# Token-major projections with a transposed hand-over in a two-layer hybrid encoder

## The chip, the core and the metric

The kernel runs on one core of a Trainium2 chip. The metric is the device time of one execution in microseconds (us); of the kernel before, three runs were timed and the median counts. The engines, as the profile names them: PE is TensorE's matrix multiply and PEld its weight load, DVE is VectorE, ACT is ScalarE, POOL is GpSimd, and SP is the queue that issues nearly all transfers.

## The reference

Two residual layers over 256 tokens of 2048 features, all in float32. Layer 0 mixes tokens by attention (16 query heads, 4 key/value heads, RMS-normed and rotated), layer 1 by a recurrence with a convolution of width 4 in front and a gate branch beside it. Behind each mixer stands a gated feed-forward with 5632 hidden features.

```python
def rms_norm(x, g):
    y = xf * lax.rsqrt(jnp.mean(xf * xf, axis=-1, keepdims=True) + EPS)
    return (y * g).astype(x.dtype)

def recurrent_mixer(h, w_in, conv_w, conv_b, w_a, b_a, w_i, b_i, lam, w_out):
    xb, yb = jnp.split(h @ w_in, 2, axis=-1)
    yb = jax.nn.gelu(yb, approximate=True)
    xb = depthwise_conv_centred(xb, conv_w, conv_b)
    h_fwd = rg_lru(xb, ..., reverse=False)
    h_bwd = rg_lru(xb, ..., reverse=True)
    return ((h_fwd + h_bwd) * yb) @ w_out

def swiglu(h, w_gate, w_up, w_down):
    return (jax.nn.silu(h @ w_gate) * (h @ w_up)) @ w_down

for i in range(2):
    x = x + mixer[i](rms_norm(x, norm_mix[i]))
    x = x + swiglu(rms_norm(x, norm_ffn[i]), w_gate[i], w_up[i], w_down[i])
```

## The kernel before

**Number format.** Each float32 operand is split into a rounded high part and the rest: `hi` and `lo` of a weight, and the two halves `xh|xl` of an activation tile (256 + 256 columns for 256 tokens). A product is hi x xh + hi x xl + lo x xh. Weights come in halves of eight 128x128 blocks (512 KB) on SP (`load_half`, L108); ScalarE casts them to `hi` (L114) and VectorE subtracts to get `lo` (L115). The pools `raw`, `hi` and `lo` hold five halves each.

**Feature-major projections.** Activations and the residual `x_sb` are stored with features on the partitions. `blocks` (L203) holds a weight block stationary and streams the activations: one matmul of 512 columns (hi by xh|xl) and one of 256 (lo by xh), whose two halves VectorE adds up (`evac`, `add_residual`). `project_sum` (L230 to L232) sums within the accumulator by three matmuls of 256; the recurrence's input projection uses it.

**Token-major projections.** `project_tokens` (L222) holds 128 tokens of the activations stationary and streams 512 weight columns. Only layer 1's down projection uses it. For that the residual is turned to token-major: 16 transposes of VectorE (L604) and 16 transfers (L608), spread through the first units of the feed-forward.

**Feed-forward.** The 44 blocks of 128 hidden features go in parts of 16, 14 and 14. `unit` makes one block: gate, scale by 1/rms, Silu, scale (GpSimd, L632), up, product. After each part its down projection adds to the residual; one unit of the next part goes ahead of it.

**Norm.** When a block of the residual is done, ScalarE scales it by the gain (L310), VectorE makes the low part (L313), GpSimd squares and sums (L322, L324). When all are done, `finish` (L333) sums over the partitions by four matmuls with ones and takes 1/rms, which is applied after the projection.

**What sets the order.** TensorE's instructions stand in the order in which the program is written. `later(t, fn)` puts a piece of small work t steps of the running projection ahead. On the other engines a scheduler orders the instructions, and tile pools set the waits.

Of the kernel before, what the change touches and what calls it, by code (L numbers as in the profile page):

```python
# [18 lines left out]
P = 128  # L19
S = 256  # L20
# [7 lines left out]
PARTS = [16, 14, 14]  # L28
HALF = 8
WIDE = 512  # L30
COMMON = {"ss", "sq", "nv", "nr", "rsq_t", "fg", "fu"}
# [4 lines left out]
FRONT = 4  # L36
HELD = 3
# [32 lines left out]
def trunk(ctx, tc, w, out):  # L70
# [10 lines left out]

    uid = [0]
# [39 lines left out]
    def out_order(src):  # L122
        both = [halves(src[j], KT) for j in range(KT)]
        return [both[j][i] for i in range(2) for j in range(FRONT)] + sum(both[FRONT:], [])

    def ffn_order(l):
        at = np.cumsum([0] + PARTS)
        units = [sum((halves(w[f"w_{m}{l}"][i], KT) for m in ("gate", "up")), []) for i in range(at[-1])]
        seq = units[: at[1]]
        for p, n in enumerate(PARTS):  # L130
            more = units[at[p + 1] : at[p + 2]] if p + 1 < len(PARTS) else []
            src = w[f"w_down{l}_{p}"]
            if l:
                down = [[(src[c, i], HALF) for c in range(4) for i in range(n // 2)]]
            else:
                down = [halves(src[j], n) for j in range(KT)]
                if not more:
                    down[:2] = [down[j][i : i + 1] for i in range(2) for j in range(2)]
            seq += more[:1] + down + more[1:]
        return sum(seq, [])  # L140
# [3 lines left out]
    order += out_order(w["w_o"]) + ffn_order(0)  # L144
    for b in range(-1, NBLK):
        xin = range(2 * b + 2, 2 * b + 4) if b + 1 < NBLK else []
        yin = range(KT + 2 * b, KT + 2 * b + 2) if b >= 0 else []
        order += sum((halves(w["w_in"][c], KT) for c in (*xin, *yin)), [])
    order += out_order(w["w_out"]) + ffn_order(1)
# [63 lines left out]
    def project_tokens(xs):  # L213
        accs = [new_acc() for _ in range(2)]
        for k0 in range(0, len(xs), 2):
            half()
# [16 lines left out]

    def project_sum(xs):
        bank = new_acc()
        acc = bank[:, :S]
        for k0 in range(0, len(xs), HALF):
            for k, (hi, lo) in enumerate(half(), k0):
                three(acc, hi, lo, xs[k], k == 0, k == len(xs) - 1)
                step()  # L240
        return acc, bank[:, S:]

    def output(xs, ready, norm, close):
        accs = [new_acc() for _ in range(FRONT)]
        for acc in accs:
            blocks(acc, half(), xs, 0)
        late = [half() for j in range(HELD)]
        for acc, wt in zip(accs, late):
            blocks(acc, wt[: ready - HALF], xs, HALF)
        flush()  # L250
        close()
        for j in range(KT):
            if j < HELD:
                blocks(accs[j], late[j][ready - HALF :], xs, ready)
            elif j < FRONT:
                blocks(accs[j], half(), xs, HALF)
            acc = accs[j] if j < FRONT else project(xs)
            add_residual(j, acc, norm)
        norm.finish_later(NORM + 2)
# [15 lines left out]
    xq = [cst.tile([P, 4, S], F32, tag=f"x{k}", name=f"x{k}") for k in range(KT // 4)]  # L275
    x_sb = [xq[k // 4][:, k % 4, :] for k in range(KT)]
# [4 lines left out]
    cn = ap.tile([P, 2 * S + P], F32, tag="cn", name="cn", bufs=1)  # L281
# [7 lines left out]
    ident = cn[:, 2 * S :]  # L289
# [6 lines left out]
    class Norm:  # L296
        def __init__(self, gname, gofs):
            self.g = (gname, gofs)
            self.xs = []
            self.ss = tmp("ss", bufs=1)  # L300

        def add(self, k):
            self.scale(k)
            self.square(k, pool)

        def scale(self, k, eng=act):
            g = col(self.g[0], self.g[1] + k)
            t = xp.tile([P, 2 * S], F32R, tag="xg", name=nm("xg"), bufs=16)
            if eng is act:
                i = act.activation(t[:, :S], x_sb[k], AF.Copy, scale=g)  # L310
            else:
                i = eng.tensor_scalar(t[:, :S], x_sb[k], g, 1.0, ALU.mult, ALU.mult)
            dve.scalar_tensor_tensor(t[:, S:], x_sb[k], g, t[:, :S].bitcast(F32), ALU.mult, ALU.subtract)  # L313
            self.xs.append(t)
            return i

        def square(self, k, eng):
            sq = self.ss if k == 0 else tmp("sq", bufs=4)
            if eng is act:
                act.activation(sq, x_sb[k], AF.Square)  # L320
            else:
                eng.tensor_tensor(sq, x_sb[k], x_sb[k], ALU.mult)  # L322
            if k:
                pool.tensor_tensor(self.ss, self.ss, sq, ALU.add)  # L324

        def finish_later(self, delay=NORM):
            later(delay, self.finish)

        def finish(self):
            pst = ps_m.tile([P, 2 * S], F32, tag="pm", name=nm("pm"))  # L330
            for a in range(2):
                sl = slice(a * P, a * P + P)
                pe.matmul(pst[:, sl], ones, self.ss[:, sl], start=True, stop=True)  # L333
            self.v = tmp("nv", bufs=1)
            dve.tensor_scalar(self.v, pst[:, :S], 1.0 / D, EPS, ALU.mult, ALU.add)
            self.r = rsqrt(self.v, "nr")
# [12 lines left out]
    def add_residual(j, acc, norm):  # L349
        dve.tensor_tensor(x_sb[j], x_sb[j], acc[:, :S], ALU.add)  # L350
        dve.tensor_tensor(x_sb[j], x_sb[j], acc[:, S:], ALU.add)
        if norm is not None:
            norm.add(j)
# [23 lines left out]
    def scale_x(i):  # L377
        for k in range(2 * i, 2 * i + 2):
            j = n0.scale(k)
            if i:  # L380
                follow(j, newest["cast"])
# [9 lines left out]
    x_tok = ap.tile([P, 2, D], F32, tag="kv", name="x_tok", bufs=1)  # L391

    def token_squares(a):
        for i in range(2):
            t = x_tok[:, a, i * D // 2 : (i + 1) * D // 2]
            newest["cast"] = follow(act.activation(t, t, AF.Square, accum_out=msq[:, a, i : i + 1]), newest["cast"])  # L396

    def load_tables():
        sync.dma_start(out=cn, in_=w["cn"])
# [61 lines left out]
    def keys_values():  # L461
        kv = ap.tile([P, 2 * NKV, 2 * S], F32R, tag="kv", name="kv", bufs=1)
        kT.extend(kv[:, h, :] for h in range(NKV))
        vt.extend(kv[:, NKV + h, :].rearrange("p (a b d) -> p a b d", a=2, b=2) for h in range(NKV))
# [123 lines left out]
    def end_attention():  # L588
        decay_constants()
        at.close()  # L590
        scope.pop()

    nf = Norm("norm_ffn", 0)
    output(o_t, KT - 2, nf, end_attention)


    class Turned:
        def __init__(self):
            fp = ctx.enter_context(tc.tile_pool(name="fp", bufs=1))
            self.blocks = fp.tile([P, 8, KT, 32], F32, tag="xb", name="xb")  # L600
            self.x = fp.tile([P, 2, 4, WIDE], F32, tag="xt", name="xt")

        def turn(self, k):
            dve.transpose(self.blocks[:, :, k, :], x_sb[k])  # L604

        def move(self, i, j):
            src = self.blocks[32 * i : 32 * i + 32, j::4, :, :].rearrange("p a k r -> p a (k r)")
            sync.dma_start(out=self.x[32 * j : 32 * j + 32, :, i, :], in_=src)  # L608

        def add(self, c, accs, end):  # L610
            for a, acc in enumerate(accs):
                n = 2 if end and c == 3 else 1
                for i in range(n):
                    sl = slice(i * WIDE // n, (i + 1) * WIDE // n)
                    y = self.x[:, a, c, sl]
                    dve.tensor_tensor(y, y, acc[:, sl], ALU.add)
                    if end:
                        sync.dma_start(out=out[:, a, c, sl], in_=y)


    def ffn(l, norm, nxt):
        turned = Turned() if nxt is None else None
        moves = []
        if turned:
            moves = [partial(turned.turn, k) for k in range(KT)]
            moves += [partial(turned.move, i, j) for i in range(4) for j in range(4)]

        def unit(i):
            g = evac(project(norm.xs), "fg")
            dve.tensor_tensor(g, g, norm.r, ALU.mult)  # L630
            table_act(g, g, AF.Silu)
            pool.tensor_tensor(g, g, norm.r, ALU.mult)  # L632
            u = evac(project(norm.xs), "fu")
            dve.tensor_tensor(u, u, g, ALU.mult)
            h = act_tile()
            split(h, u)
            return h

        bounds = np.cumsum([0] + PARTS)
        hid = []  # L640
        for i in range(PARTS[0]):
            hid.append(unit(i))
            if i >= 2:
                for _ in range(3):
                    if moves:
# [237 lines left out]
```

## Time and profile before

| | |
|---|---|
| runs | 2060.05, 2060.22, 2060.23 us, median 2060.22 |
| profiled execution | 2060.85 us, its span 2059.1 us |
| granted TensorE clock | 1.00 |
| busy share PE, DVE, ACT, POOL | 100%, 69%, 52%, 19% |
| moved from and to memory | 388 MB, 189 GB/s |

The profile is one execution. Busy time is the time in which an engine executed something; the chain of waits follows the work that ended last backwards, so that its shares add up to the span. A row such as `L203 PE MATMUL ... x3200 | 1011.1, 395 | 0.3` gives line, engine, operation, count, busy time in us, mean of one in ns, and the idle time of the engine ahead of it. Matmuls overlap in their pipeline, so their pace is read from a stretch of them divided by their number, not from the mean of one.

### The profile page before, as it was taken

The numbers are of one execution on the slowest core, as the hardware profiler recorded it, in microseconds if no ns is written. First come the engines' busy times: TensorE is split into PE (matmuls) and PEld (weight loads), VectorE is DVE, ScalarE is ACT, GpSimd is POOL, SyncE is SP. The second block draws the span as 40 slices with busy tenths as digits, with TensorE's granted clock in tenths as the row PEclk, the third lists the DMA queues.
The fourth block names the chain that finished last, engine by engine and source line by source line (L and its number), as shares of the span: only waits on it lengthen the run. The fifth ranks groups of instructions, "written<-read, shape, count | busy, mean of one in ns | idle before, by whom it ended". The sixth has DMA issues, their size and how long they took to land.

```text
span 2059.1 us, 32056 instructions
## 1 busy us (share of the span) xinstructions
PE 2051.9 (100%) x12162; PEld 1812.3 (88%) x12162; DVE 1428.1 (69%) x2093; ACT 1069.0 (52%) x1597; POOL 391.1 (19%) x394
## 2 busy tenths in 40 slices
PE   9999999999999999999999999999999999999999
PEld 8898888888888888888999998888888888888887
DVE  7998876665566666668878879866654666556654
ACT  7666444443344434444589896544443444444442
POOL 1563611110011000113334433311100111001100
PEclk9999999999999999999999999999999999999999
DMA  8444655555555565556555545665555555555553
GB/s 315 160 137 140 223 189 187 192 185 193 186 191 187 177 193 200 187 181 185 199 177 178 193 149 197 203 215 190 189 193 195 186 191 187 194 194 185 190 201 130
DMA packets 111306, 388.43 MB, mean 189 GB/s; under 512 B 12592, under 2 KB 13232, under 8 KB 111024
## 3 DMA queue, kind: packets, MB, share of 16 engines
q1 hardware_dynamic: 111008, 386.36, 56.4%
q8 instruction: 96, 1.57, 0.3%
q14 instruction: 58, 0.48, 0.1%
q10 hardware_dynamic: 144, 0.02, 0.0%
HBM read 382.13 MB, written 2.10 MB: 187 GB/s over the span
## 4 chain that ended last, share of the span: by engine, by line
PE 95%; DVE 2%; DMA 1%; ACT 1%; issue 1%; POOL 0%; SPq 0%; DVEq 0%; POOLq 0%
PE acc L203 71%; PE acc L222 12%; PE acc L230 3%; PE acc L231 3%; PE acc L232 3%; PE pm L232 1%; DVE lo L115 1%; PE pm L230 1%; PE pm L231 1%; DMA x_tok<-in_xt_dram 1%; DMA raw<-in_w_k_dram 0%; PE pm L539 0%; ACT hi L114 0%; ACT x_tok L396 0%; PE pm L511 0%
## 5 line engine op out<-in xcount | busy, mean ns | idle before, releaser
L115 DVE TENSOR_TENSOR lo<-raw,hi 128x1024 fp32r<-128x1024 f32 (+1 forms) x716 | 885.3, 1237 | 384.7 <-ACT hi L114 378.7
L114 ACT CAST hi<-raw 128x1024 fp32r<-128x1024 f32 (+1 forms) x716 | 740.4, 1036 | 582.5 <-PE acc L203 265.7
L203 PE MATMUL acc<-xg,hi 128*128 128x512 f32 x3200 | 1011.1, 395 | 0.3 <-ACT hi L114 0.3
L203 PEld LDWEIGHTS acc<-xg,lo 128*128 128x128 f32 x3200 | 600.9, 188 | 141.1 <-DVE lo L115 2.2
L203 PE MATMUL acc<-xg,lo 128*128 128x256 f32 x3200 | 638.4, 279 | 0.7 <-DVE lo L115 0.6
L203 PEld LDWEIGHTS acc<-xg,hi 128*128 128x128 f32 x3200 | 489.9, 189 | 0.8 <-ACT hi L114 0.6
L203 PE MATMUL acc<-act,hi 128*128 128x512 f32 x1202 | 379.0, 395 | 0.0
L632 POOL TENSOR_TENSOR fg<-fg,nr 128x256 f32<-128x256 f32 x88 | 118.1, 1342 | 1182.6 <-ACT fg L364 1182.6
L203 PEld LDWEIGHTS acc<-act,lo 128*128 128x128 f32 x1202 | 225.8, 188 | 52.9
L203 PE MATMUL acc<-act,lo 128*128 128x256 f32 x1202 | 237.3, 278 | 0.0
L222 PE MATMUL acc<-hi,act 128*128 128x512 f32 x704 | 217.3, 389 | 0.0
L203 PEld LDWEIGHTS acc<-act,hi 128*128 128x128 f32 x1202 | 183.6, 189 | 0.0
L222 PEld LDWEIGHTS acc<-hi,act 128*128 128x128 f32 x704 | 132.1, 188 | 27.3
L230 PE MATMUL acc<-xg,hi 128*128 128x256 f32 x512 | 144.8, 283 | 0.0
L231 PE MATMUL acc<-xg,hi 128*128 128x256 f32 x512 | 144.6, 282 | 0.0
L232 PE MATMUL acc<-xg,lo 128*128 128x256 f32 x512 | 144.4, 282 | 0.0
L222 PE MATMUL acc<-lo,act 128*128 128x512 f32 x352 | 136.9, 389 | 0.0
L263 ACT COPY fg<-acc 128x256 f32<-128x256 f32 x88 | 32.8, 373 | 150.0 <-PE acc L203 149.8
L263 ACT COPY fu<-acc 128x256 f32<-128x256 f32 x88 | 32.8, 372 | 149.4 <-PE acc L203 149.4
L232 PEld LDWEIGHTS acc<-xg,lo 128*128 128x128 f32 x512 | 97.9, 191 | 0.0
L230 PEld LDWEIGHTS acc<-xg,hi 128*128 128x128 f32 x512 | 97.9, 191 | 0.0
L231 PEld LDWEIGHTS acc<-xg,hi 128*128 128x128 f32 x512 | 97.9, 191 | 0.0
(180 smaller groups left out, 1595.6 us busy)
## 6 DMA issues: line engine op xcount, KB each, us to landing
raw<-in_w_gate_dram SPq DMA_DIRECT2D x176, 512.0 KB, 3.4
raw<-in_w_up_dram SPq DMA_DIRECT2D x176, 512.0 KB, 3.4
raw<-in_w_down_dram SPq DMA_DIRECT2D x152, 512.0 KB, 3.3
raw<-in_w_in_dram SPq DMA_DIRECT2D x64, 512.0 KB, 4.0
raw<-in_w_qv_dram SPq DMA_DIRECT2D x40, 512.0 KB, 3.5
raw<-in_w_o_dram SPq DMA_DIRECT2D x32, 512.0 KB, 4.2
raw<-in_w_out_dram SPq DMA_DIRECT2D x32, 512.0 KB, 3.6
raw<-in_w_down_dram SPq DMA_DIRECT2D x32, 384.0 KB, 3.1
```

The costliest lines, as they stand in the source:

```text
L114: newest["cast"] = act.copy(hi[:, sl, :], raw[:, sl, :])
L115: dve.tensor_tensor(lo[:, sl, :], raw[:, sl, :], hi[:, sl, :].bitcast(F32), ALU.subtract)
L203: pe.matmul(o, w, x, start=(k == 0 and not part), stop=(k == total - 1 and not part))
L222: pe.matmul(accs[a], x, wt[:, k, :], start=(k0 + k == 0 and n == 0), stop=(end and k == 1 and n == 2))
L230: pe.matmul(o, hi, x[:, :S], start=start, stop=False)
L231: pe.matmul(o, hi, x[:, S:], start=False, stop=False)
L232: pe.matmul(o, lo, x[:, :S], start=False, stop=stop)
L263: i = act.copy(t, acc[:, S:])
L632: pool.tensor_tensor(g, g, norm.r, ALU.mult)
```

## The change

The residual `x_tok` is kept token-major throughout, and w_o, w_out, gate, up and down of both layers all go through `project_tokens` (L223 in the new file) in four, or eleven, columns of 512 features. Whatever has to be an operand of the next projection is brought back to features by `turned`: for 512 columns two transposes of 32x32 blocks on VectorE and 16 transfers from on-chip memory to on-chip memory of 32 KB, all on SP, or half on ScalarE's queue for the last columns ahead of a norm (`hurry`). The hidden features come out of a unit four blocks at a time, and the parts are 12, 16 and 16 blocks; no unit goes ahead of a down projection. The sums of squares are ScalarE's, by token; 1/rms goes into the Silu's scale and into the product. Only the recurrence's input projection stays feature-major, and needs 1/rms along the columns: `spread` multiplies a diagonal by ones. Its first two projections are interleaved (`project_two`), so that the last four operands come late in both.

```diff
-PARTS = [16, 14, 14]
+PARTS = [12, 16, 16]
...
+    def project_two(xs, late):
+        banks = [new_acc() for _ in range(2)]
+        for t in banks:
+            sums(t[:, :S], half(), xs, 0)
+        rest = [half() for _ in range(2)]
+        n = len(xs) - HALF - late
+        for t, wt in zip(banks, rest):
+            sums(t[:, :S], wt[:n], xs, HALF)
+        for t, wt in zip(banks, rest):
+            sums(t[:, :S], wt[n:], xs, HALF + n)
+            yield t[:, :S], t[:, S:]
...
+        def operand(self, x, wide=False):
...
+            i = act.activation(hi, x, AF.Copy, scale=g)
+            dve.scalar_tensor_tensor(lo, x, g, hi.bitcast(F32), ALU.mult, ALU.subtract)
...
+        def add(self, c):
+            for a in range(2):
+                act.activation(tmp("nj", (P, WIDE), bufs=1), x_tok[:, a, c, :], AF.Square, accum_out=self.sums[:, a, c : c + 1])
+            for f in turned(x_tok[:, :, c, :], c == NCOL - 1):
+                self.operand(f, True)
...
+        def spread(self):
+            dg = tmp("ndg", bufs=1)
             for a in range(2):
+                dve.tensor_scalar(dg[:, a * P : (a + 1) * P], ident, self.rt[:, a : a + 1], None, ALU.mult)
+
+            def stage():
+                pst = ps_m.tile([P, 2 * S], F32, tag="pm", name=nm("pm"))
+                for a in range(2):
+                    sl = slice(a * P, a * P + P)
+                    pe.matmul(pst[:, sl], ones, dg[:, sl], start=True, stop=True)
+                self.r = tmp("nrb", bufs=1)
+                act.copy(self.r, pst[:, :S])
+
+            later(NORM, stage)
...
+    def turned(src, hurry=False):
+        b = fp[0].tile([P, 2, FOUR, P], F32, tag="tb", name=nm("tb"))
+        f = fp[0].tile([P, 8, FOUR, 32], F32, tag="tf", name=nm("tf"))
+        for a in range(2):
+            dve.transpose(b[:, a, :, :], src[:, a, :])
+        for q in range(4):
+            for i in range(4):
+                (act if hurry and i % 2 else sync).dma_start(
+                    out=f[32 * i : 32 * i + 32, q::4, :, :].rearrange("f a k t -> f a (k t)"),
+                    in_=b[32 * q : 32 * q + 32, :, i, :],
+                )
+        return [f[:, :, k, :] for k in range(FOUR)]
...
+    def output(xs, norm=None, end=False, ready=0, close=None):
+        for c in range(NCOL):
+            accs = project_tokens(xs, ready, None if c else close)
...
+        def unit():
+            g, u = (fp[0].tile([P, 2, WIDE], F32, tag=t, name=nm(t), bufs=1) for t in ("fg", "fu"))
+            for a, acc in enumerate(project_tokens(norm.xs)):
+                table_act(g[:, a, :], acc, AF.Silu, scale=norm.rt[:, a : a + 1])
+            for a, acc in enumerate(project_tokens(norm.xs)):
+                dve.scalar_tensor_tensor(u[:, a, :], acc, norm.rt[:, a : a + 1], g[:, a, :], ALU.mult, ALU.mult)
+            for f in turned(u):
+                h = act_tile()
+                hi, lo = (h[:, o : o + S].rearrange("p (q t) -> p q t", t=32) for o in (0, S))
+                act.copy(hi, f)
+                dve.tensor_tensor(lo, f, hi.bitcast(F32), ALU.subtract)
+                yield h
+
         for p, n in enumerate(PARTS):
+            hid = [h for _ in range(n // FOUR) for h in unit()]
             last = p == len(PARTS) - 1
...
+            output(hid, nxt if last else None, last and nxt is None)
...
+            accs = (project_sum(nr.xs) for _ in range(2)) if blk else project_two(nr.xs, FOUR)
+            nxt.xcs = [conv_branch(2 * b + 2 + i, t) for i, t in enumerate(accs)]
```

The first place is the start of the recurrence. On VectorE (DVE) the rows before, around the step that turns the norm's sum `pm` into 1/rms `nr` (L335 to L346) and the first use of it in the convolution (L685), were these:

```order
L665 TENSOR_TENSOR x_78<-x_78,acc_10068 128x256
L115 TENSOR_TENSOR lo_10334<-raw_10332,hi_10333 128x1024
L313 SCALAR_TENSOR_TENSOR xg_10124<-x_78,pk,xg_10124 128x256
L335 TENSOR_SCALAR nv_10192<-pm_10189 128x256
L115 TENSOR_TENSOR lo_10364<-raw_10362,hi_10363 128x1024
L344 TENSOR_TENSOR rsq_t_10195<-nv_10192,nr_10194 128x256
L345 SCALAR_TENSOR_TENSOR rsq_t_10195<-rsq_t_10195,nr_10194 128x256
L346 SCALAR_TENSOR_TENSOR nr_10194<-rsq_t_10195,nr_10194 128x256
L685 TENSOR_TENSOR cb_10222<-acc_10149,nr_10194 128x256
```

In the changed kernel the last residual column's two transposes (L348) are followed by the norm's small steps, the low parts of the four operands `xg` made from the transferred `tf`, and the diagonal `ndg`:

```order
L117 TENSOR_TENSOR lo_8876<-raw_8874,hi_8875 128x1024
L322 TENSOR_REDUCE nrt_8665<-nsq_3258 128x2
L323 TENSOR_SCALAR nrt_8665<-nrt_8665 128x2
L117 TENSOR_TENSOR lo_8906<-raw_8904,hi_8905 128x1024
L368 TENSOR_TENSOR rsq_s_8669<-nrt_8665,nr_8668 128x2
L308 SCALAR_TENSOR_TENSOR xg_8653<-tf_8634,pk,xg_8653 128x256
L308 SCALAR_TENSOR_TENSOR xg_8656<-tf_8634,pk,xg_8656 128x256
L308 SCALAR_TENSOR_TENSOR xg_8659<-tf_8634,pk,xg_8659 128x256
L369 SCALAR_TENSOR_TENSOR rsq_s_8669<-rsq_s_8669,nr_8668 128x2
L308 SCALAR_TENSOR_TENSOR xg_8662<-tf_8634,pk,xg_8662 128x256
L370 SCALAR_TENSOR_TENSOR nr_8668<-rsq_s_8669,nr_8668 128x2
L330 TENSOR_SCALAR ndg_8676<-ident,nr_8668 128x128 x2
```

So 1/rms comes ahead of the matmuls of L336 and behind the four operands, where it came after the matmuls of L333 and apart from the operands. On TensorE the two matmuls of L336 stand 27 matmuls into the interleaved projections, at the same distance as L333 before:

```order
L231 MATMUL acc_8699<-xg_8101,hi_8731 128x256
L232 MATMUL acc_8699<-xg_8101,hi_8731 128x256
L233 MATMUL acc_8699<-xg_8101,lo_8732 128x256
L336 MATMUL pm_8739<-ndg_8676,ones 128x128 x2
L231 MATMUL acc_8699<-xg_8104,hi_8731 128x256
```

The second place is the first down projection of layer 0. On SP the 16 transfers `tf` of the part's last unit stand among the loads of the down weights, ten halves behind the last half of the up weights:

```order
L110 DMA raw_4363<-in_w_down_0_dram 128x1024
L110 DMA raw_4381<-in_w_down_0_dram 128x1024
L110 DMA raw_4399<-in_w_down_0_dram 128x1024
L110 DMA raw_4417<-in_w_down_0_dram 128x1024
L351 DMA tf_4218<-tb_4217 32x2x128 x16
L110 DMA raw_4435<-in_w_down_0_dram 128x1024
```

Before, SP had nothing but weight loads there. On TensorE the first operand `act_4237` made from them is used in the fifth half of the down weights, behind the eight operands of the two units ahead (here the end of the fourth):

```order
L223 MATMUL acc_4250<-hi_4306,act_3916 128x512
L223 MATMUL acc_4250<-lo_4307,act_3916 128x512
L223 MATMUL acc_4250<-hi_4306,act_3916 128x512
L223 MATMUL acc_4249<-hi_4324,act_4237 128x512
L223 MATMUL acc_4249<-lo_4325,act_4237 128x512
```

More of the change, by code (lines that the diff above doesn't have):

```diff
@@ L34 @@
 GRID_W = 64
-FRONT = 4
-HELD = 3
 WARM = 10
@@ L147, in trunk @@
         yin = range(KT + 2 * b, KT + 2 * b + 2) if b >= 0 else []
-        order += sum((halves(w["w_in"][c], KT) for c in (*xin, *yin)), [])
-    order += out_order(w["w_out"]) + ffn_order(1)
+        both = [halves(w["w_in"][c], KT) for c in (*xin, *yin)]
+        order += [t[i] for i in range(2) for t in both] if b < 0 else sum(both, [])
+    order += wide("w_out") + ffn_order(1)
     taken = [0]
@@ L232, in three, with sums @@
         pe.matmul(o, lo, x[:, :S], start=False, stop=stop)
+    def sums(acc, wt, xs, k0):
+        for k, (hi, lo) in enumerate(wt, k0):
+            three(acc, hi, lo, xs[k], k == 0, k == len(xs) - 1)
+            step()
     def project_sum(xs):
         bank = new_acc()
-        acc = bank[:, :S]
         for k0 in range(0, len(xs), HALF):
[L238 to L259, printed above, removed]
+            sums(bank[:, :S], half(), xs, k0)
+        return bank[:, :S], bank[:, S:]
+    def project_two(xs, late):
[9 more added lines that the diff above has]
+            yield t[:, :S], t[:, S:]
     def evac(acc, tag, after=None):
@@ L299, in __init__ @@
             self.xs = []
[L300 to L307, printed above, removed]
-            t = xp.tile([P, 2 * S], F32R, tag="xg", name=nm("xg"), bufs=16)
[L309 to L313, printed above, removed]
+            self.sums = tmp("nsq", (P, 2, NCOL))
@@ L591, in end_attention @@
         scope.pop()
+        open_ffn()
     nf = Norm("norm_ffn", 0)
[L594 to L618, printed above, removed]
@@ L621, in ffn @@
[L621 to L645, printed above, removed]
-                        moves.pop(0)()
+    output(o_t, nf, ready=KT - 2, close=end_attention)
```

169 lines of the change are left out of this document (78 added, 91 removed).

## The prediction

> **What bounds the kernel now.** I read the page first, for the engine that is never idle:
>
> ```profile
> PE 2051.9 (100%) x12162; PEld 1812.3 (88%) x12162; DVE 1428.1 (69%) x2093; ACT 1069.0 (52%) x1597; POOL 391.1 (19%) x394
> PEclk9999999999999999999999999999999999999999
> PE 95%; DVE 2%; DMA 1%; ACT 1%; issue 1%; POOL 0%; SPq 0%; DVEq 0%; POOLq 0%
> ```
>
> TensorE is busy in all of the span at the full clock, and the chain that ended last is 95% TensorE. So only the number and the pace of its matmuls count, until something makes it wait. The chain in order of time (start, length, what, how many instructions) gives the paces, and one window inside the recurrence the third:
>
> ```profile
> 273.46 0.44 PE pm L333 x4
> 273.90 726.99 PE acc L203 x4174
> ...
> 1514.83 87.06 PE acc L222 x384
> ...
> 1979.01 76.18 PE acc L222 x336
> ```
>
> ```profile
> 1060.00:1180.00 120.00, 120.00 (x1007) 120.00 (x1006) 102.44 (x167) 109.19 (x186) 45.48 (x58) 1.00 0.57 185
> ```
>
> L203 is the feature-major projection: per 128x128 weight block one matmul of 512 columns and one of 256, 2 x 726.99/4174 = 348.3 ns. L222 is the token-major one: 87.06/384 = 226.7 ns per matmul of 512. Four blocks side by side (128x512 weights) take three of them for each 128 of the 256 tokens, so six: 1.5 a block, 340.1 ns. The piece at 1979.01 agrees (76.18/336 = 226.7). The recurrence's input projection takes three matmuls of 256: 3 x 120.00/1007 = 357.5 ns. None of these stretches has a gap: 726.99 us of back-to-back matmuls cross every boundary between projections of layer 0. That is what the change puts at stake.
>
> **What TensorE gains.** Changed blocks: w_o 256, w_out 256, gate and up of both layers 2 x 1408, the down projection of layer 0 704: 4032, of which 14 (its last column) went by three matmuls of 256. 4018 x (348.3 - 340.1) = 33.2 us, 14 x 17.4 = 0.2 us, and two of the three sums over features (0.44 us each) go: 0.9 us. Together **34.3 us**, and this term is firm, since both paces are measured in long stretches.
>
> **What the new path costs.** Each 512 columns now pass through two residual or multiply operations, two transposes, 16 transfers, then scale or copy on ScalarE and a subtraction on VectorE. Before, the next operand needed only a few VectorE steps. The rows:
>
> ```profile
> L616 DVE TENSOR_TENSOR xt<-xt,acc 128x512 f32<-128x512 f32 x22 | 14.0, 680 | 0.0
> L604 DVE STREAM_TRANSPOSE xb<-x 128x256 f32<-128x256 f32 x16 | 7.1, 442 | 0.4
> L115 DVE TENSOR_TENSOR lo<-raw,hi 128x1024 fp32r<-128x1024 f32 x678 | 851.9, 1257 | 360.2 <-ACT hi L114 354.3
> L114 ACT CAST hi<-raw 128x1024 fp32r<-128x1024 f32 x678 | 711.2, 1050 | 536.0 <-PE acc L203 239.2 <-issue 156.3 <-PE acc L222 133.1
> L310 ACT ACTIVATE xg<-x,pk 128x256 fp32r<-128x256 f32 x64 | 31.4, 504 | 13.4 <-DVE x L351 11.3 <-DMA pk<-in_pk_dram 1.9
> L690 DVE SCALAR_TENSOR_TENSOR acc<-cb,pk,acc 128x256 f32<-128x256 f32 x32 | 15.4, 482 | 0.4
> L542 ACT CAST pT<-pm 128x256 fp32r<-128x256 f32 x32 | 11.8, 368 | 11.3 <-PE pm L539 9.4 <-DVE pT L543 1.9
> L364 ACT ACT_TABLE_LOAD x38 | 48.8, 1283 | 0.7
> ```
>
> A transpose of 512 is not there; between 0.44 and twice that I take 0.71 us, near L616's time for the same size. For the transfers the nearest rows are the 16 of layer 1, 32 x 2 x 512 where the new ones are 32 x 2 x 128: the view of tile xt, the timeline, the DMA issues, and line 108's weight loads beside them (ns as minimum, median, maximum).
>
> ```profile
> L608 SPq DMA_DIRECT2D xt<-xb x16: 591/595/1934, 1326.4 to 1340.6; - x16
> ...
> DMA to landing us min/median/max: 1.8/5.0/7.4
> ```
>
> ```profile
> 1336.81 1.87 SPq L608 DMA_DIRECT2D xt<-xb  x3
> ```
>
> ```profile
> xt<-xb SPq DMA_DIRECT2D x16, 128.0 KB, 5.6
> ```
>
> ```profile
> L108 SPq DMA_DIRECT2D raw<-in_w_down_dram x184: 327/328/340, 436.9 to 2030.4; - x184
> ```
>
> An issue holds SP's queue 0.595 us, and three in a row took 1.87: I take 0.635 each; the lower bound is a weight load's issue, 0.33, with the same gap 0.37. For the landing of the last one I take 2.4 us, nearer to the 1.8 (nothing else is then in flight) than to the median 5.6 for four times the bytes beside weight loads.
>
> *The chain of a feed-forward unit* (four blocks of features), from E, the end of its last up matmul: multiply 0.68 for the second half of the tokens (the first half's sum is done 1.4 us sooner), transpose 0.71, a weight split that stands between 1.26, transpose 0.71, four handovers that I estimate at 0.1: 3.8 us. Fifteen issues: 13.3. Landing: 15.7. ScalarE's copy 0.37 and a handover: the first operand is ready at **E + 16.2**. SP's later weight loads wait behind the 16 issues (10 us, under four of the 2.72 us that 12 matmuls of 227 ns take); five buffers and the order put them later than that, so I cost this at nothing.
>
> When does TensorE ask? Parts are now 12, 16, 16 blocks. In a part of 16, 12 blocks come from earlier units, six groups of 12 matmuls: E + 16.3. Four such boundaries, and two at the first gate after a norm, are just in time; in sum I put **2.0 us** on them. In the parts of 12 only eight blocks, four groups, lie ahead: E + 10.9, a stall of 5.3 us, twice.
>
> *What a stall does to the clock.* The start and the end of the trace show it: two timelines of TensorE, and two windows (the number before the last two is the granted clock).
>
> ```profile
> 0.99 4.63 PE L287 MATMUL pm<-ones 128*128 128x128 f32 x20 [0.99 <-POOL ones L284]
> ```
>
> ```profile
> 2054.78 0.39 PE L222 MATMUL acc<-hi,act 128*128 128x512 f32 x1
> ```
>
> ```profile
> 2057.00:2058.00 1.00, 0.00 (x0) 0.00 (x0) 0.00 (x0) 0.00 (x0) 0.00 (x0) 0.83 0.37 126
> 2058.00:2059.10 1.10, 0.00 (x0) 0.00 (x0) 0.00 (x0) 0.00 (x0) 0.00 (x0) 0.50 0.00 0
> ```
>
> The 128-column matmuls of the start take 4.63/20 = 231 ns against 0.44/4 = 110 at 273.46: half speed, for some 5 us. The last matmul ends at 2055.2, and the granted clock is 0.83 in the slice from 2057 and 0.50 in the next. So a stall over about 2.5 us ends at half clock, and 5 us at half speed lose **2.5 us**. Bounds: nothing, or all of it.
>
> The Trainium skill ("TensorE: Matmul & The Clock Gate", Part 1) has a window of about 3.4 us of idleness for the drop and as much of work for the return. By that a restart loses 1.7 us, and the sum below comes out 2.8 us lower; the trace's start took longer, and I keep its number.
>
> So the two parts of 12 cost 2 x (5.3 + 2.5) = **15.6 us**.
>
> *The start of the recurrence.* In the new instruction order there stands, 27 matmuls of 119 ns after the feed-forward's end, a pair of matmuls that spreads the norm's 1/rms over the partitions (where L333 stood: hidden before, since its sum came column by column). Now it needs the per-token 1/rms, and on VectorE the diagonal stands behind the four operands of the last 512 columns. The chain from E: residual 0.68, two transposes and a weight split in progress, 3.4; ScalarE issues half the transfers, 8 x 0.635: 8.5; table load 1.28 and logarithm: 10.0; a weight cast 1.05: 11.0; table load and exponential: 12.5; four scalings of 0.50, the last with VectorE's 0.48 behind it: 15.0; two small steps and the diagonal: 15.8. TensorE is there at 3.2: idle **12.6 us**, with the clock **15.1**. From below I bound it by the transfers alone (landed at 3.4 + 7 x 0.635 + 2.4 = 10.3, one scaling and the diagonal: idle 8), from above by one table load and one cast more, 15.
>
> Behind it, the first two convolution branches now end 12 matmuls (1.4 us) apart instead of 48 (5.7). Each takes VectorE about 3.3 us:
>
> ```profile
> L685 DVE TENSOR_TENSOR cb<-acc,nr 128x256 f32<-128x256 f32 x16 | 6.6, 415 | 1.0 <-PE acc L232 0.9
> L687 ACT ACTIVATE acc<-cb,pk 128x256 f32<-128x256 f32 x16 | 9.1, 567 | 4.0 <-DVE cb L685 4.0
> L271 DVE TENSOR_TENSOR xs<-xc,xs 128x256 fp32r<-128x256 f32 x16 | 9.8, 610 | 0.5
> L270 DVE CAST xs<-xc 128x256 fp32r<-128x256 f32 x16 | 13.2, 828 | 0.3
> ```
>
> (0.42 + 3 x 0.48 + 0.83 + 0.61). Two of them with three weight splits are 10.4 us; the first gate matmul comes 54 matmuls, 6.4 us, after the second sum. Stall some 4.4 us (bounds 0 to 6), and 1.5 for the clock: **5.9 us**.
>
> At the end of attention TensorE meets the last two heads' operands once, under the same schedule of small work as before; two blocks are one group of 12 matmuls, so the cost lies between 0 and 2.7 us, and since the schedule is kept I take **0.5 us**. The kernel's end is as before. GpSimd loses its multiplications and squares; it was 19% busy and nobody's bound: nothing.
>
> **The sum.** 15.6 + 2.0 + 15.1 + 5.9 + 0.5 = 39.1 us against 34.3: 4.8 us slower. The profiled execution took 2060.85 us (span 2059.1 and 1.75 around it), 0.63 above the median 2060.22 of the runs: 2065.6 there, **2065.0** as a median. Differences under 0.2% (4.1 us) count as none in what follows.
>
> **Rivals.** *The issues are cheap* (0.37 us, the pattern's rows being short): the last one of a unit starts at E + 9.4, its operand is ready at E + 12.2, the two stalls shrink from 5.3 to 1.3 and the clock stays up: 13.0 us less. The just-in-time places cost nothing (2.0), and the recurrence starts 8 x 0.265 = 2.1 sooner: **2047.9**. For it: the weight load's row. Against: L608's 591 ns is a minimum, in the same form.
>
> *The clock holds through stalls of 5 us*: 9.0 us less (three times 2.5, and 1.5), **2056.0**. Against: the end of the trace.
>
> *The transfers wait for each other.* Every issue names one of eight completion counters and waits until the transfer eight places earlier has landed. Above 8 x 0.635 = 5.1 us of landing the counters set the pace. At the row's median of 5.6 us it is 0.70 a transfer, 1.0 us more at each of six unit boundaries: **2071**. At its maximum, 7.4 us, it is 0.93: 4.4 us at all six, and the four of 16 blocks lose the clock as well, 6 x 4.4 + 4 x 2.5: **2101**. For it: the row's landing times. Against: a quarter of the bytes. [...]
>
> **Chances.** The forecast's mechanism 0.45, cheap issues 0.20, a clock that holds 0.15, waiting transfers 0.20. Faster by over 0.2%: cheap issues 0.20 and half of the held clock 0.08: 0.28. Within 0.2%: the other half 0.07, and of the forecast the part in which the branches or the spread come some 1 us or more sooner, 0.17: 0.24. Slower: the rest of the forecast 0.28 and the waiting transfers 0.20: 0.48. The range goes from the cheap issues to the waiting transfers at about 6.4 us of landing, and leaves out half of each: 2048 to 2080.
>
> **What would show it.** In the profile after: L223 at 227 ns in long pieces; TensorE idle some 5 us in the first down projection of each feed-forward; one gap of 10 us or more ahead of the spread at L336, with a granted clock of 0.5 behind it; the issues of L351 at 0.6 us. I am wrong if those issues take under 0.45 us, if the granted clock stays full, or if TensorE waits somewhere that I have as just in time.

## The result and the profile after

The changed kernel takes 2062.49 us (median of 20 runs, 2059.90 to 2068.08) against 2060.22 before (20 runs): ratio 1.0012, 95% interval 1.0005 to 1.0019. It is slower by 2.3 us, 0.1%, within the 0.2% that the prediction counts as none. The forecast was 2065.0. The runs before lie within 1.0 us of each other; those after are spread over 8.2.

The profiled execution took 2061.56 us, its span 2059.8 (before: 2059.1). Its page:

```profile
PE 2026.1 (98%) x10124; PEld 1725.6 (84%) x10124; DVE 1239.0 (60%) x1627; ACT 1057.4 (51%) x1506; POOL 166.5 (8%) x213
...
PEclk9999999999999999999899999999999999999999
...
PE 86%; DVE 4%; SPq 4%; DMA 3%; ACT 1%; issue 1%; ACTq 0%; POOL 0%; DVEq 0%
```

TensorE was busy 100% before and is 98% now; its share of the chain fell from 95% to 86%, and SP's queue, which had 0%, holds 4%. So work was taken off TensorE and waits took its place. The matmuls' gain, from the chain in order of time:

```profile
194.69 200.65 PE acc L223 x885
```

226.7 ns a matmul, as L222 had. The waits of TensorE in the changed kernel (who was waited for, us in total, times, the longest):

```profile
PE pm L336 <- DVE ndg L330: 14.1, 1, 14.1
PE acc L223 <- ACT act L643: 9.2, 2, 4.6
PE pm L232 <- DVE xs L269: 1.0, 2, 0.6
```

Three places carry it: the spread at the recurrence's start, the two first down projections, the first gate matmuls. Between the start of one matmul and that of the next the two down projections lose 4.75 us each.

*The first down projection.* Its piece of the chain (the 16 issues all alike; most are left out) is the predicted one step by step:

```profile
398.91 0.30 DVE tb L348
...
399.54 1.18 DVE lo L117
400.72 0.63 DVE tb L348
...
401.37 0.59 SPq L351
401.96 0.05 issue
402.01 0.59 SPq L351
...
410.96 1.88 DMA tf<-tb
...
413.06 0.41 ACT act L643
413.47 0.04 issue
413.52 6.70 PE acc L223 x22
```

A transpose, the weight split that stands between, the other transpose, then issues every 0.64 us, the last one's landing 1.88, a cast 0.41. TensorE's timeline has the last up matmul (on `xg`) and the first down matmul (on `act`):

```profile
397.66 0.39 PE L223 MATMUL acc<-hi,xg 128*128 128x512 f32 x1
397.88 0.39 PE L223 MATMUL acc<-hi,act 128*128 128x512 f32 x1
```

So E is 397.9, and the operand is used at 413.5: E + 15.6, where E + 16.2 was forecast.

*The clock.* Windows of the same trace, the granted clock third from the end:

```profile
409.00:414.00 5.00, 0.48 (x1) 0.49 (x2) 1.73 (x3) 1.95 (x5) 0.00 (x0) 0.92 0.40 85
414.00:417.00 3.00, 3.00 (x9) 2.32 (x9) 0.93 (x3) 0.38 (x2) 0.00 (x0) 0.56 1.02 414
1011.00:1013.00 2.00, 2.00 (x12) 2.00 (x11) 0.00 (x0) 0.62 (x1) 0.15 (x1) 0.50 0.42 151
1476.00:1480.00 4.00, 4.00 (x10) 3.10 (x10) 1.05 (x4) 0.50 (x2) 0.00 (x0) 0.50 1.02 390
```

After each stall the clock is at half for some microseconds: by the excess of the matmuls' starts over their usual spacing, 1.5 us lost behind the first down projection of layer 0, 2.7 behind that of layer 1, 2.4 behind the spread.

### The profile page after: what moved, and what is told of

Same layout as the page of the kernel before. It is cut to its first block, busy times and chain, and to the rows that moved or that the text cites. A ratio compares the mean times of both kernels' runs of the same rounds, so it can differ in the third digit from the quotient of the medians.

```text
span 2059.8 us, 27679 instructions
## 1 busy us (share of the span) xinstructions
PE 2026.1 (98%) x10124; PEld 1725.6 (84%) x10124; DVE 1239.0 (60%) x1627; ACT 1057.4 (51%) x1506; POOL 166.5 (8%) x213
## 4 chain that ended last, share of the span: by engine, by line
PE 86%; DVE 4%; SPq 4%; DMA 3%; ACT 1%; issue 1%; ACTq 0%; POOL 0%; DVEq 0%
PE acc L223 70%; PE acc L201 5%; SPq L351 3%; PE acc L231 3%; PE acc L232 3%; PE acc L233 3%; DVE lo L117 2%; PE pm L233 1%; PE pm L232 1%; PE pm L231 1%; DMA raw<-in_w_down_dram 1%; ACT hi L116 1%; DMA raw<-in_w_in_dram 1%; DMA raw<-in_w_k_dram 0%; DMA graw<-in_w_gates_dram 0%
## 5 line engine op out<-in xcount | busy, mean ns | idle before, releaser
L223 PE MATMUL acc<-hi,xg 128*128 128x512 f32 x2816 | 868.2, 389 | 0.7 <-ACT xg L307 0.7
L223 PEld LDWEIGHTS acc<-hi,xg 128*128 128x128 f32 x2816 | 528.6, 188 | 111.0 <-ACT xg L307 1.1
L223 PE MATMUL acc<-hi,act 128*128 128x512 f32 x1920 | 598.3, 391 | 9.2 <-ACT act L643 9.2
L223 PE MATMUL acc<-lo,xg 128*128 128x512 f32 x1408 | 547.8, 389 | 0.4 <-DVE lo L117 0.4
L223 PEld LDWEIGHTS acc<-hi,act 128*128 128x128 f32 x1920 | 362.4, 189 | 85.8 <-ACT act L643 10.2
L223 PE MATMUL acc<-lo,act 128*128 128x512 f32 x960 | 375.1, 391 | 0.0
L223 PEld LDWEIGHTS acc<-lo,xg 128*128 128x128 f32 x1408 | 264.3, 188 | 55.5 <-DVE lo L117 0.9
L223 PEld LDWEIGHTS acc<-lo,act 128*128 128x128 f32 x960 | 181.4, 189 | 37.1
L233 PE MATMUL acc<-xg,lo 128*128 128x256 f32 x512 | 145.2, 284 | 0.0
L201 PE MATMUL acc<-xg,hi 128*128 128x512 f32 x384 | 126.0, 397 | 0.4 <-ACT hi L116 0.4
L231 PEld LDWEIGHTS acc<-xg,hi 128*128 128x128 f32 x512 | 98.8, 193 | 0.0
L232 PEld LDWEIGHTS acc<-xg,hi 128*128 128x128 f32 x512 | 98.7, 193 | 0.0
L233 PEld LDWEIGHTS acc<-xg,lo 128*128 128x128 f32 x512 | 98.7, 193 | 0.0
L201 PE MATMUL acc<-xg,lo 128*128 128x256 f32 x384 | 84.7, 288 | 0.2 <-DVE lo L117 0.2
L201 PEld LDWEIGHTS acc<-xg,lo 128*128 128x128 f32 x384 | 72.2, 189 | 15.1 <-DVE lo L117 0.9
L201 PEld LDWEIGHTS acc<-xg,hi 128*128 128x128 f32 x384 | 60.9, 189 | 0.8 <-ACT hi L116 0.7
L399 ACT ACT_TABLE_LOAD x38 | 48.8, 1283 | 14.1 <-DMA tf<-tb 13.5
```

What stands on the lines that cost most here:

```text
L201: pe.matmul(o, w, x, start=(k == 0 and not part), stop=(k == total - 1 and not part))
L223: pe.matmul(accs[a], x, wt[:, k, :], start=(k0 + k == 0 and n == 0), stop=(end and k == 1 and n == 2))
L231: pe.matmul(o, hi, x[:, :S], start=start, stop=False)
L232: pe.matmul(o, hi, x[:, S:], start=False, stop=False)
L233: pe.matmul(o, lo, x[:, :S], start=False, stop=stop)
L399: table_op(act.activation(*a, **k))
```

## The experiments

The theory: the matmuls' gain of 34 us is given back at a few places where the transposed hand-over lasts longer than the work that covers it, with the half clock behind each. Its rivals: the landing of the transfers rather than their issue, VectorE and ScalarE alone, or a cost that lies elsewhere. Times are medians; the changed kernel's 2062.49 is the reference, so a difference of 2 or 3 us stands against its own spread of 8.2. The kernel before, timed again beside each experiment, kept its median within 0.5 us (2060.14 to 2060.63).

**e4, no transfers.** The operands are read from the transposed blocks as they lie.

```diff
-        for q in range(4):
-            for i in range(4):
-                (act if hurry and i % 2 else sync).dma_start(...)
-        return [f[:, :, k, :] for k in range(FOUR)]
+        v = b.rearrange("p a k f -> p (a k f)")
+        return [v[:, k * S : (k + 1) * S].rearrange("p (q t) -> p q t", t=32) for k in range(FOUR)]
```

> All 544 transfers are left out; the next operands are read from the transposed blocks as they lie, so their content is not the projection's. If the transfers are the cost: both stalls of the feed-forward go (9.5 us and 4.2 of clock), the recurrence's start loses the 6.4 us of issues and the landing (some 7 us), and the slips ahead of the feed-forwards (1.7) go: some 22 us less, about 2040. If VectorE's transposes and ScalarE's casts already cost most of it: 5 us less or under, about 2058.

Measured 2037.1 (2036.3 to 2037.8), 25.4 less. In its waits the down projections are gone and the spread's wait is down to 5.7:

```profile
PE pm L336 <- DVE ndg L330: 5.7, 1, 5.7
```

So the transfers are 25 of the 35 us lost; what is left is at the recurrence's start, VectorE and ScalarE ahead of the spread, the slower matmuls behind it and the first gate matmuls.

**e9, issues doubled.** Sixteen more transfers, into a tile nobody reads, ahead of the last unit's sixteen in each first part.

```diff
+        if twice:
+            e = fp[0].tile([P, 8, FOUR, 32], F32, tag="te", name=nm("te"), bufs=1)
+            for q in range(4):
+                for i in range(4):
+                    sync.dma_start(out=e[32 * i : 32 * i + 32, q::4, :, :]..., in_=b[32 * q : 32 * q + 32, :, i, :])
```

> Ahead of the 16 transfers of the last unit of each first part stand 16 more, from the same blocks into a tile that nobody reads; nothing else changes. If the time that SP's queue is held per issue sets the stall: it grows by 10 to 11 us at both places, from 4.75 to 15, and the time to about 2083. If the landing sets it (the transfers overlap, and the queue only pipelines them): it grows by 2 to 4 us, 2067 to 2071.

One run, 2079.6, and its waits and SP's timeline:

```profile
PE acc L223 <- ACT act L651: 29.6, 2, 14.8
```

```profile
401.66 10.19 SPq L353 DMA_DIRECT2D te<-tb  x16
411.89 10.18 SPq L359 DMA_DIRECT2D tf<-tb  x16
```

Sixteen issues hold the queue 10.2 us, and each wait grew by 10.2. Here it is the issue that is paid, not the landing. From span to span the total grew by 18.0 (2059.8 to 2077.8), not by 20.4: in this execution the spread waited 1.1 us less (13.0) and the wait at the start of the second feed-forward was 0.7 smaller; the last 0.6 is not accounted for, with one run.

**e5, one unit ahead.** The first unit of the second part goes before the first part's down projection (weights in that order).

```diff
-            for _ in range(n // FOUR):
+            for _ in range(n // FOUR + (1, -1, 0)[p]):
...
+        hid = []
         for p, n in enumerate(PARTS):
-            hid = [h for _ in range(n // FOUR) for h in unit()]
+            hid += [h for _ in range(n // FOUR + (1, -1, 0)[p]) for h in unit()]
...
-            output(hid, nxt if last else None, last and nxt is None)
+            cur, hid = hid[:n], hid[n:]
+            output(cur, nxt if last else None, last and nxt is None)
```

> One unit of the second part (43 us of TensorE) goes ahead of the first part's down projection, in both layers; nothing else changes. If the wait at the parts of 12 is only the short cover of eight blocks: both stalls of 4.75 us and the half clock behind them (1.5 and 2.7 us) go, the time falls by 13.7 to about 2049, and no new wait appears. If the transfers delay the weight loads behind them on SP, which the stall has hidden: TensorE waits for a weight split instead, and the time falls by less than 7 us, 2056 or more.

Measured 2048.35, ratio to the kernel before 0.9942 (0.9929 to 0.9956), 14.1 less than the changed kernel. The chain runs in one piece past the first down projection of layer 0:

```profile
194.97 746.22 PE acc L223 x3291
```

So the short cover of eight blocks was the cause of both stalls, and the loads that queue behind the sixteen issues cost nothing.

**e2, two queues at those places.** The last unit of each first part issues half of its transfers on ScalarE's queue.

```diff
-            for f in turned(u):
+            for f in turned(u, hurry):
...
-            hid = [h for _ in range(n // FOUR) for h in unit()]
+            hid = [h for i in range(n // FOUR) for h in unit(not p and i == n // FOUR - 1)]
```

> The last unit of the first part of each feed-forward issues half of its 16 transfers on ScalarE's queue. If SP's 16 issues of 0.635 us set the stall of 4.75 us there: the issues take 5.1 us instead of 10.2, the operand is ready before TensorE asks for it, the two stalls and the clock loss behind them go, 2 x 4.75 + 1.5 + 2.7 = 13.7 us, about 2049. If the two queues share one generator of descriptors, or the landing sets the pace: the stalls stay, about 2062.

Measured 2062.12, no gain. SP's and ScalarE's timelines:

```profile
402.66 6.76 SPq L351 DMA_DIRECT2D tf<-tb  x8
```

```profile
402.67 7.09 ACTq L351 DMA_DIRECT2D tf<-tb  x8
409.88 2.94 ACT L116 CAST hi<-raw 128x1024 fp32r<-128x1024 f32 x3 [6.73 <-DMA tf<-tb]
412.72 1.32 ACT L643 CAST act<-tf 128x256 fp32r<-128x256 f32 x4
```

Sixteen issues are done in 7.1 us instead of 10.2, and not in 5.1. A single issue is no slower: on ScalarE's queue it takes (minimum, median and maximum in ns)

```profile
L351 ACTq DMA_DIRECT2D tf<-tb x40: 592/611/862, 273.5 to 1470.3; - x40
```

But both queues stand still for 1.7 us in the middle. Every issue waits for the landing eight places back, as the prediction's third rival has it, and the trace shows the same eight counters in the issues of both queues. So ScalarE's fourth issue, due at 404.82, starts at 406.56, when a weight load that SP had issued ahead of the transfers has landed (406.54), and SP's next starts when one of ScalarE's first transfers has. The chain shows the second:

```profile
402.67 4.24 DMA tf<-tb
406.90 0.02 issue
406.92 0.58 SPq L351
```

Besides, ScalarE casts nothing while it issues, and in its order three weight casts, 2.94 us, then stand ahead of the operands. The operands' casts start 10.0 us after the first issue; with one queue it was 11.7. By the starts of the matmuls the stalls of 4.75 us shrink to 3.1 and 2.4, but a new one of 1.1 us follows each, for the operands' low parts, which on VectorE now stand behind three weight splits:

```profile
PE acc L223 <- DVE act L644: 1.9, 2, 0.9
```

So the landing holds the issues, as the second expectation had it (1.7 us), and the casts and splits that were put off take most of the rest. Of the 1.8 us that the waits still save, the median shows 0.4.

**e1, matmuls that keep the clock.** Matmuls of ones by ones fill the waits.

```diff
+    def fill(n):
+        t = ps_m.tile([P, P], F32, tag="pm", name=nm("pm"))
+        for _ in range(n):
+            pe.matmul(t, ones, ones, start=True, stop=True)
...
-            output(hid, nxt if last else None, last and nxt is None)
+            first = not p
+            output(hid, nxt if last else None, last and nxt is None, n - FOUR if first else 0, partial(fill, 20) if first else None)
...
             def stage():
+                fill(60)
                 pst = ps_m.tile([P, 2 * S], F32, tag="pm", name=nm("pm"))
```

> 20 fp32 matmuls of ones by ones (4.4 us) are put ahead of the fifth half of the first down projection of each layer, and 60 (13.1 us) ahead of the spread at the recurrence's start, into accumulators that nobody reads. If the idle time is what lowers the clock: the granted clock stays at 1.0 over all three places, the excess of the matmuls behind them (1.5, 2.7 and 2.4 us in the changed kernel's trace) goes, and the time falls by some 6.6 us from 2062.5 to about 2056. If the lower clock does not come from the idle time, or the places end later for another reason: no change, 2062.5, or more by what the added matmuls overrun.

Measured 2060.40 (ratio to before 1.0001, 0.9993 to 1.0010): 2.1 less than the changed kernel instead of 6.6. The windows that stood at 0.56 and 0.50 are at full clock:

```profile
414.00:417.00 3.00, 2.52 (x11) 2.02 (x12) 1.43 (x4) 1.33 (x4) 0.00 (x0) 1.00 0.89 332
...
1011.00:1013.00 2.00, 2.00 (x19) 2.00 (x18) 0.00 (x0) 1.96 (x3) 1.28 (x2) 1.00 0.03 10
```

Idle time is what lowers the clock; that part is shown. That it paid only a third has two causes in the profile. The wait ahead of the first gate matmuls grew from 2.4 to 4.3 us: with its clock kept TensorE is 3 us sooner there, and VectorE's convolution ends only some 1 us sooner. And in this execution the sixteen issues took 11.1 us instead of 10.2, so the down projections still waited behind the filling:

```profile
401.38 11.14 SPq L352 DMA_DIRECT2D tf<-tb  x16
```

```profile
PE acc L223 <- ACT act L649: 2.0, 2, 1.1
```

In that group one issue took 1.55 us, although the counter it waits for was free; why single issues sometimes take so long stays open. It may be part of the spread between the runs of the changed kernel, which was not tested.

**e3, the spread later.** The spread comes behind both interleaved projections.

```diff
-            later(NORM, stage)
+            later(31, stage)
...
-            nxt.xcs = [conv_branch(2 * b + 2 + i, t) for i, t in enumerate(accs)]
+            nxt.xcs = [conv_branch(2 * b + 2 + i, t) for i, t in enumerate(accs if blk else list(accs))]
```

> The matmuls that spread 1/rms come behind the two interleaved projections of the recurrence's start instead of 27 matmuls into them. If the spread alone holds TensorE: it goes on to the last four operands, 72 matmuls or 8.6 us after the feed-forward's end instead of 3.2, and waits there until they are ready at some 15, so the idle time falls from 14.1 to about 6.5, and the convolution starts some 10 us sooner: 7 to 10 us less, 2053 to 2055. If the convolution's VectorE work behind it is what ends last: the wait moves to the first gate matmul and the time stays within 3 us of 2062.5.

Measured 2059.61, 2.9 less: by its time the second expectation, by its waits some of both. The wait at the spread turned into one for the last operands and one at the first gate matmul:

```profile
PE acc L231 <- ACT xg L307: 7.7, 1, 7.7
PE pm L231 <- issue: 2.8, 1, 2.8
```

So the spread is not alone: both it and the operands hang on ScalarE's queue, and VectorE's convolution ends late behind them.

**e6, branches apart.** `project_sum` in place of `project_two`.

```diff
-        order += [t[i] for i in range(2) for t in both] if b < 0 else sum(both, [])
+        order += sum(both, [])
...
-            accs = (project_sum(nr.xs) for _ in range(2)) if blk else project_two(nr.xs, FOUR)
+            accs = (project_sum(nr.xs) for _ in range(2))
```

> The first two projections of the recurrence run one after the other (project_sum, weights in that order) instead of interleaved; the spread stays 9 steps in. If interleaving is what brings the convolutions late: the waits ahead of the first gate matmuls (2.4 us) go, the 14.1 us ahead of the spread stay, about 2060. If these waits come from the late start of VectorE as a whole: they stay, 2062.5.

Measured 2059.61, 2.9 less. The spread waits 13.9 as before, and no wait for `xs` is left:

```profile
PE pm L336 <- DVE ndg L330: 13.9, 1, 13.9
```

The interleaving costs those 2.4 us; and since the spread blocks TensorE 27 matmuls in, long before the late operands are asked for, it gives nothing back.

**e7, one queue at the recurrence's start.**

```diff
-            for f in turned(x_tok[:, :, c, :], c == NCOL - 1):
+            for f in turned(x_tok[:, :, c, :], c == NCOL - 1 and self.g != ("norm_mix", KT)):
```

> The last 16 transfers ahead of the recurrence all go by SP; ScalarE issues none there. If ScalarE's own queue (8 issues ahead of the logarithm and the exponential) holds the spread: 1/rms is ready some 9.5 us after the feed-forward's end instead of 17, the operands at about 16.4; TensorE idles 6 us ahead of the spread and 1 to 2 ahead of the last operands instead of 14.1, some 6 us less, 2056. If the landing of the transfers holds it: SP's 16 issues take 10.2 us instead of 6.4, and the time grows by 3 to 4, 2066.

Measured 2057.36, ratio to before 0.9985 (0.9976 to 0.9993), 5.1 less. In the changed kernel ScalarE's timeline, and in this one:

```profile
996.09 6.35 ACTq L351 DMA_DIRECT2D tf<-tb  x8
1002.48 1.28 ACT L399 ACT_TABLE_LOAD   x1 [6.71 <-DMA tf<-tb]
```

```profile
997.38 1.03 ACT L116 CAST hi<-raw 128x1024 fp32r<-128x1024 f32 x1
998.43 1.28 ACT L399 ACT_TABLE_LOAD   x1
```

```profile
PE pm L336 <- DVE ndg L330: 5.1, 1, 5.1
...
PE pm L232 <- DVE xs L269: 2.7, 2, 2.1
```

The logarithm no longer waits behind eight issues, and the spread waits 5.1 us instead of 14.1, though the transfers take longer. The eight issues were put on ScalarE to bring the operands sooner; they held up 1/rms, which TensorE meets first. Of the 9 us at the spread only 5.1 reach the time. TensorE comes sooner to the first gate matmuls and waits longer there for VectorE's `xs`: by the starts of the first 60 of them 6.5 us are lost, with the lower clock, where it was 2.6.

**e8, e5 and e7 together.**

> Both edits together, one unit ahead of the first down projection and the last transfers ahead of the recurrence on SP alone. If the two places are independent, the gains add: 13.7 and 6, about 2043, faster than both kernels. If the clock's window or a shared queue ties them: less than 13 together, 2050.

Measured 2044.07, ratio 0.9924 (0.9909 to 0.9939): 18.4 less than the changed kernel, where the two alone gave 14.1 and 5.1. The places are all but independent.

**e10, the last transfers split behind the exponential.** As e8, but 5 of the 16 on ScalarE's queue, held behind the exponential; for that the norm's `finish` is written ahead of the transfers.

```diff
+            if hurry and self.g == ("norm_mix", KT):
+                self.finish()
+                hurry = 5
...
+                by_act = 4 * q + i >= 16 - hurry if hurry == 5 else hurry and i % 2
+                d = (act if by_act else sync).dma_start(...)
+                if hurry == 5 and by_act:
+                    follow(d, prev[0])
```

> One unit ahead of the first down projection, and ahead of the recurrence 11 of the last 16 transfers on SP and 5 on ScalarE's queue, placed behind the logarithm and the exponential. If the last operands' transfers still hold TensorE after the spread: they land some 3 us sooner than with SP alone, and the time falls by up to 3 from 2044.1, to 2041. If VectorE's convolution work ends last there: what is gained goes to the wait ahead of the first gate matmuls, 2044.

Measured 2039.44 (2038.1 to 2041.0), ratio 0.9899 (0.9881 to 0.9916): 1% faster than before. Its waits:

```profile
PE pm L340 <- DVE ndg L334: 5.4, 1, 5.4
PE pm L232 <- DVE xs L269: 1.1, 1, 1.1
PE pm L231 <- DVE xs L268: 1.1, 1, 1.1
```

In e8 the wait for the last operands was 0.6 us and the largest at the first gate matmuls this:

```profile
PE pm L232 <- DVE xs L269: 3.4, 2, 2.1
```

The wait for the last operands is gone, and the waits at the first gate matmuls fell from 3.8 to 2.2 in all. So the gain over e8 is 4.6 and not the 3 at most that were expected: with the operands some 2.5 us sooner after the feed-forward's end, VectorE's convolution ends sooner as well. What is left is the spread, 5.4 us of residual, squares, table loads and the diagonal, and those 2.2.

## Why the prediction was right, and where it was off

**The gain.** Forecast 34.3 us. The new losses in the changed kernel's trace, by the starts of its matmuls, sum to 34.9 us (below); the attention, which the change hardly touches, was 0.6 us shorter in that execution, and the span grew by 0.7: 34.9 - 0.6 - 0.7 = 33.6. The pace of 226.7 ns carried over to every projection.

**The two parts of 12.** Forecast 2 x (5.3 + 2.5) = 15.6; measured 2 x 4.75 and 1.5 + 2.7 of clock, 13.7. The issue price of 0.635, the step most in doubt, was 0.64 in one queue; e9 shows that it sets the wait. The landing, taken at 2.4, was 1.9, which is most of the 0.55 by which each stall was too long. The rival of cheap issues fell with the row: 585 ns at the least, 595 in the median. So did, at these boundaries, that of transfers that wait for each other: landing takes 1.9 us in the median and 4.3 at most, under the 5.1 from which the counters decide for one queue.

**The start of the recurrence.** Forecast 12.6 + 2.5; measured 14.1 + 2.4. Two terms were small. The feed-forward ends at 991.7 and the transposes at 996.1, 4.3 us later and not 3.4:

```profile
991.73 0.28 PE L231 MATMUL acc<-xg,hi 128*128 128x256 f32 x1
```

```profile
994.77 1.30 DVE L348 STREAM_TRANSPOSE tb<-x_tok 128x512 f32<-128x512 f32 x2
```

And ScalarE's eight issues took 6.35 us and not 5.1. The chain shows where 1.0 us of that went: the fourth issue, due at 998.24, started only when a weight load issued ahead of the transfers had landed.

```profile
993.68 5.55 DMA raw<-in_w_in_dram
999.23 0.02 issue
999.25 0.59 ACTq L351
```

So here, for 1.0 us, the rival of waiting transfers came true. It was reckoned with one queue; when two issue at once and share the eight counters, eight places pass in some 8 x 0.32 = 2.6 us (an estimate from issues 0.64 apart on each), and this weight load took 5.55 to land. The mechanism, issues ahead of two table loads on ScalarE, is shown by e7.

**The convolutions behind it.** Forecast 5.9; measured 2.6. This is the term that was most off in size. (Its own numbers, 10.4 less 6.4, give 4.0 and not the 4.4 written.) It was worked out as if TensorE ran at the full clock up to there, while its half clock was charged to the spread as well: the 2.4 us lost before cover part of the wait. e1 shows the exchange: with the clock kept, the wait rose to 4.3, near the 4.4 of the forecast, and over the first 60 gate matmuls, the lower clock behind the wait included, 5.8 us were lost. The two costs overlap, and I had added them.

**Just in time, and the end of attention.** Forecast 2.0 and 0.5; measured 1.7, all at the feed-forward of layer 1, none at the four boundaries of 16; and 0.4.

In sum 39.1 forecast, 34.9 measured in the profile: 13.7 + 16.5 + 2.6 + 1.7 + 0.4. That 2065.0 lies 2.5 us from 2062.49 owes something to luck, since the time is a small difference of two large sums: the costs came out 4.2 us too high and the gain 0.7 too low, the spread too low and the convolutions too high, and from one profiled execution to the other the kernel lost 0.7 us where 4.8 were forecast. By the prediction's own measure the result, 0.1% slower, is no difference at all, a case to which it gave 0.24, against 0.48 for slower; the branches that end their waits sooner, its main reason for that case, are what the trace shows. The rival that the clock holds is refuted by the windows at 0.50 to 0.56. "TensorE: Matmul & The Clock Gate" in the Trainium skill (Part 1) would have had, by estimate from its window, 1.7 us per restart; the three were 1.5, 2.7 and 2.4, so its number is nearer to one and the start of the trace to two.

## What to carry to other kernels

When a kernel is bound by one engine without a gap, a faster form of its work is worth its pace only if every hand-over still fits under work that does not need it; count that cover at each boundary, in time, from the issue of the first transfer to the last. Sixteen small transfers cost what issuing them takes. Lending them to a second queue holds up whatever stands behind them in that engine's order, here the very step that was needed first, and makes both queues wait sooner for a late landing. Where a stall is followed by a half clock, do not add the next wait to it without asking whether the slow stretch already covers it.

## What the runs showed that was not expected

Two queues that issued at once did not halve the time, though no single issue was slower (medians of 595 and 611 ns): both wait on the same eight counters, and one late landing stops both. That cost 1.7 us in e2 and 1.0 at the recurrence's start of the changed kernel. An issue on ScalarE's queue holds what stands behind it, not what has begun: in e10 two issues, from 992.30, ran beside ScalarE's table load of 992.28 to 993.56. A single issue can also last up to 1.85 us without such a landing; the cause stays open. And a kernel with stalls repeats worse: 8.2 us between its fastest and slowest run, where the kernel before had 1.0.
